# A diffusion step with an S5 scan, a long convolution and a pooling branch: squares summed on TensorE, one normalisation pass over all tokens, filter bias by matmul, and convolution tiles spread evenly beside the scan

## The chip, the cores and the metric

The kernel runs on one core of a Trainium2 chip. The metric is the device time of one execution in microseconds. The kernel before took 1530.49 us, the median of three runs (1528.8 to 1534.48).

## What is computed

One inference step runs 640 tokens (512 latent, 128 context) of width 1024 through two layers. Latents and context have their own conditioning vectors, but share all weights. In outline, for each layer:

```
shift, scale, gate = split(silu(cond) @ w_mod + b_mod)
h = rms_norm(x, norm_g) * (1 + scale) + shift
u_a, g_a, u_b, g_b, u_c, g_c, m = split(h @ w_in)
y_a = glu(gelu(s5_bidirectional(u_a))) * silu(g_a)
y_b = hyena(u_b) * silu(g_b)
y_c = pool(u_c) * silu(g_c)
x = x + gate * ((sigmoid(m_a) * (y_a @ w_br_a) + sigmoid(m_b) * (y_b @ w_br_b)
                 + sigmoid(m_c) * (y_c @ w_br_c)) @ w_out)
```

`hyena` first runs a three-tap convolution over u_b, which gives v, x1 and x2, and then twice z = gate * (long convolution of z with filter h_o, plus z * bias). The filters h_o come from a small MLP over positions, `sin` twice, times a decaying window. `s5_bidirectional` is a complex diagonal recurrence in both directions with 32 groups of 16 channels and 64 states. A final RMS norm ends the step.

## The kernel before

All of it is in fp32 precision: matmuls with the weights W = wh + wl and the data h = hhi + hlo are made of three products in a rounded fp32 form (lines 261 to 263). `split()` makes such a pair: ScalarE rounds (line 238) and VectorE subtracts (line 239). `linear()` streams a weight tile of 128 output channels from memory over SP's DMA queue in two pieces of 256 KB (`wr`), splits each piece, and multiplies with both halves of 320 tokens.

The program is one Python order of calls, from which a scheduler of the framework makes one in-order queue for each engine; it may pull independent instructions of later calls ahead. The stages are:

- **Prologue.** `run()` loads the S5 parameters, runs the filter MLP, computes the S5 discretisation on VectorE (`s5_disc`), squares x0 (`square()`: ScalarE squares a tile, VectorE adds it to an accumulator, line 589), loads the filter's matrices, and makes the modulation in four chunks (`mod_chunk` and `mod_turn`, order 2, 3, 0, 1: chunks 2 and 3 are the scale, 0 and 1 the shift, each for four of the eight channel tiles). A chunk reads 2 MB of w_mod through four buffers `wm` of 512 KB, so four buffers are one chunk. `rinv()` sums the accumulators on TensorE with a column of ones (`ssq`, line 599), takes 1/sqrt by Newton steps on tiny 64x10 tiles, and spreads the result over partitions with a diagonal tile `rdg` and a matmul `rbc`. `make_h()` then makes h: `ht` = x * scale * rr (line 661), `hhi` on ScalarE (line 664), `hlo` on VectorE (line 665); channel tiles 3 and 6 begin on GpSimd (line 656). The half of 320 tokens that holds the boundary of latents and context is done in pieces of 192 and 128. Four calls of `filter()` make the spectra of the long convolution's filters: a matmul over the MLP's output (`fw`, `fwp`), the window (lines 520, 521), the bias added to one row of `hx` and one of `hq` (lines 522, 523), a fold (lines 555 to 559), and matmuls with DFT matrices (`fps`) whose results go to memory (`hd`).
- **Scan stage**, in `layer()`. `u_a` computes the scan's input. Then for each of 8 blocks, `s5_gen` makes matrices: GpSimd and VectorE build `i0`, `i1`, `ow` (lines 873 to 875), TensorE makes `khp` (line 904), ScalarE and VectorE move it to `kh` (lines 906, 907), which goes to memory as `kd` and comes back in a shifted layout as `mt` (line 914). `s5_run` runs the recurrence (`z`, `kk`, `w` on VectorE) and multiplies with `mt` and `ow` into `yp` (lines 974, 976). After each block 3 or 2 tiles of a list `beside` are taken: twelve `conv_u` (TensorE's projection, a copy to `raw`, two VectorE passes of 642 columns, lines 1003 and 1005), four `gate_b` (a gate tile, then two multiplies on GpSimd, line 1034) and four `ahead` (gates put aside in memory). So convolutions fill blocks 0 to 4 (3, 2, 3, 2, 2 of them), and blocks 5 to 7 have none.
- The GLU, four Hyena long convolutions with the pooling branch, the merge of the branches (`merge`, `merge2`), and the output projection.
- **Layer boundary.** Beside the output projection of layer 0 the filters of layer 1 are made; then `rinv` with its Newton steps on GpSimd, `make_h` in two halves, the last two filters, and the `u_a` of layer 1. `s5_vals` clears the tiles `bp` and `bf` (lines 832 and 835) on VectorE.

Of the kernel before, what the change touches and what calls it, by code (L numbers as in the profile page):

```python
# [51 lines left out]
C_ID, C_ONE, C_MT, C_CM, C_DM, C_SEL, C_POSR, C_POSC, C_EL, C_ER, C_PI2, C_EPS, C_MAG, C_N = range(14)  # L52


def _cst_layout():
    sizes = [P, P, NA + NBW, CZ, H, 2, 4 * 8, 4 * 64, 15, 11, 1, 1, 1]
# [166 lines left out]
class Body:  # L223
# [264 lines left out]
    def filter(self, l, o, hf, F, buf=None):  # L488
# [121 lines left out]
    def rinv(self, halves, e, tag="b", root=False):  # L610
# [34 lines left out]
    def make_h(self, l, X, half, rr):  # L645
        nc = self.nc
        sm, sg = self.smod[l]
        t0 = half * HT
        for kk in range(KD):
            t = self.N.tile([P, HT], F32, tag="ht", name="ht", bufs=2)  # L650
            for s, e, _, ci in self.segs(half):
                b = sm[:, kk, ci:ci + 1]
                hi = self.hhi[:, kk, t0 + s:t0 + e]
                lo = self.hlo[:, kk, t0 + s:t0 + e]
                if kk in (3, 6):
                    nc.gpsimd.tensor_tensor(out=t[:, s:e], in0=X[:, kk, t0 + s:t0 + e], in1=rr[:, s:e], op=ALU.mult)
                    nc.scalar.activation(t[:, s:e], t[:, s:e], AF.Identity, scale=sg[:, kk, ci:ci + 1], bias=b)
                    nc.scalar.copy(hi, t[:, s:e])
                    nc.vector.tensor_tensor(out=lo, in0=t[:, s:e], in1=hi.bitcast(F32), op=ALU.subtract)  # L659
# [848 lines left out]
```

## Time and profile before

| | us |
|---|---|
| median of three runs | 1530.49 |
| lowest, highest | 1528.8, 1534.48 |
| the profiled execution | 1534.17 |
| its span in the profile | 1532.4 |
| TensorE busy | 1435.3 (94%) |
| VectorE busy | 1125.5 (73%) |
| ScalarE busy | 672.0 (44%) |
| GpSimd busy | 524.9 (34%) |

The profiled execution is 3.7 us above the median of the runs. Engines are called PE (TensorE), DVE (VectorE), ACT (ScalarE), POOL (GpSimd) and SP (SyncE, which issues the DMAs) in the rows. TensorE's busy share is 94% over the whole, but busy time counts a matmul at half clock as well as one at full clock, and it is not spread evenly: the first 100 us, the two scan stages (about 120 to 340 and 875 to 1090 us) and the layer boundary (800 to 870 us) hold most of what is not busy or runs at a lower granted clock.

### The profile page before, as it was taken

Reading aid. Unit: us, or ns where it says so; the run is one execution under the profiler, and the core shown is the slowest. Engines: PE = TensorE matmul, PEld = TensorE weight load, DVE = VectorE, ACT = ScalarE, POOL = GpSimd, SP = SyncE. Lnnn points to the kernel's source line nnn. Section 1 sums busy time; section 2 is a strip of 40 time slices with the busy share of each in tenths; the row PEclk is TensorE's granted clock in tenths of the full one; section 3 lists DMA queues with packets and bytes.
Section 4 is the critical chain, followed back from the end, with each engine's and each line's share of the span. In section 5 each row is a group of like instructions: output and inputs, shape, how many; then the busy total and the mean of one; then the engine's idle time right before and its main releaser. Section 6 shows DMA issues by size and latency. Waiting matters only on the chain.

```text
span 1532.4 us, 28365 instructions
## 1 busy us (share of the span) xinstructions
PE 1435.3 (94%) x10812; PEld 1372.2 (90%) x10812; DVE 1125.5 (73%) x1951; ACT 672.0 (44%) x1454; POOL 524.9 (34%) x473
## 2 busy tenths in 40 slices
PE   3998899999999999999998897989999999999997
PEld 1688888999999998999997787989999999999996
DVE  8996998854777795555678879896557778866665
ACT  3574545434333342344345644544443334344443
POOL 0033433500343334553323733443003444166401
PEclk9899999999999999999998899999999999999998
DMA  9535122244322246444752342223622223322154
GB/s 313 188 112 132 57 72 70 71 146 123 99 71 77 76 134 234 157 151 139 230 159 81 110 113 68 71 71 94 172 89 81 83 70 106 115 83 83 35 178 153
DMA packets 120464, 178.74 MB, mean 117 GB/s; under 512 B 33944, under 2 KB 58152, under 8 KB 119817
## 3 DMA queue, kind: packets, MB, share of 16 engines
q1 hardware_dynamic: 115737, 170.58, 36.5%
q0 software_dynamic: 1152, 5.77, 1.1%
q8 instruction: 85, 1.39, 0.4%
q10 hardware_dynamic: 3440, 0.59, 0.2%
q14 instruction: 50, 0.41, 0.1%
HBM read 152.71 MB, written 24.18 MB: 115 GB/s over the span
## 4 chain that ended last, share of the span: by engine, by line
PE 68%; DVE 15%; DMA 6%; issue 5%; ACT 3%; SPq 2%; POOL 1%; POOLq 0%; ACTq 0%; DVEq 0%
PE mm L261 15%; PE mm L263 15%; PE mm L262 15%; PE mm L333 3%; PE mm L335 3%; PE mm L334 3%; DVE wl L239 2%; PE inva L1145 1%; SPq L914 1%; DVE i L874 1%; PE invb L1145 1%; PE yp L976 1%; PE modp L404 1%; DVE vx L1003 1%; DVE hlo L665 1%
## 5 line engine op out<-in xcount | busy, mean ns | idle before, releaser
L261 PE MATMUL mm<-hhi,wh 128*128 128x320 f32 x1408 | 446.1, 318 | 15.3 <-ACT raw L996 9.0
L263 PE MATMUL mm<-hhi,wl 128*128 128x320 f32 x1408 | 440.4, 314 | 8.5 <-DVE wl L239 6.3
L262 PE MATMUL mm<-hlo,wh 128*128 128x320 f32 x1408 | 442.4, 314 | 0.5 <-DVE hlo L659 0.4
L239 DVE TENSOR_TENSOR wl<-wr,wh 128x512 fp32r<-128x512 f32 x316 | 265.9, 843 | 114.4 <-ACT wh L238 111.5
L238 ACT CAST wh<-wr 128x512 fp32r<-128x512 f32 x316 | 195.5, 619 | 269.1 <-PE mm L262 188.9
L261 PEld LDWEIGHTS mm<-hhi,wh 128*128 128x128 f32 x1408 | 269.9, 192 | 20.8 <-ACT raw L996 10.0
L263 PEld LDWEIGHTS mm<-hhi,wl 128*128 128x128 f32 x1408 | 269.5, 192 | 9.5 <-DVE wl L239 6.8
L262 PEld LDWEIGHTS mm<-hlo,wh 128*128 128x128 f32 x1408 | 270.1, 192 | 1.7 <-DVE hlo L659 1.2
L262 PE MATMUL mm<-mlo,wh 128*128 128x320 f32 x256 | 79.6, 312 | 0.5 <-DVE mlo L242 0.4
L261 PE MATMUL mm<-mhi,wh 128*128 128x320 f32 x256 | 79.1, 312 | 0.5 <-ACT wh L238 0.4
L263 PE MATMUL mm<-mhi,wl 128*128 128x320 f32 x256 | 78.8, 309 | 0.4 <-DVE wl L239 0.4
L873 POOL TENSOR_TENSOR ow<-cw,po 128x512 f32<-128x512 f32 x32 | 41.9, 1328 | 96.6 <-PE yp L976 96.5
L875 POOL TENSOR_TENSOR i<-i,i 128x1024 f32<-128x1024 f32 x16 | 40.5, 2529 | 100.6 <-DVE i L873 71.8
L1244 DVE SCALAR_TENSOR_TENSOR mth<-mth,mm 128x320 f32<-128x320 f32 x64 | 31.1, 486 | 52.5 <-PE mm L263 52.5
L1246 POOL TENSOR_TENSOR macc<-macc,mth 128x320 f32<-128x320 f32 x32 | 35.0, 1099 | 86.4 <-DVE mth L1244 86.4
L239 DVE TENSOR_TENSOR wl<-ws,wh 128x512 fp32r<-128x512 f32 x48 | 42.7, 889 | 29.7 <-ACT wh L238 28.6
L333 PE MATMUL mm<-hhi,wh 128*128 128x320 f32 x192 | 59.9, 312 | 0.0
L335 PE MATMUL mm<-hhi,wl 128*128 128x320 f32 x192 | 59.4, 309 | 0.0
L334 PE MATMUL mm<-hlo,wh 128*128 128x320 f32 x192 | 59.4, 309 | 0.0
L238 ACT CAST wh<-ws 128x512 fp32r<-128x512 f32 x48 | 29.8, 621 | 60.2 <-PE mm L334 32.3
L1052 POOL TENSOR_TENSOR ps<-pu 128x663 f32<-128x663 f32 x8 | 12.3, 1540 | 120.4 <-ACT pu L1045 120.4
L1246 POOL TENSOR_TENSOR acc<-acc,mth 128x320 f32<-128x320 f32 x32 | 37.7, 1179 | 44.4 <-DVE mth L1244 44.3
(421 smaller groups left out, 3809.9 us busy)
## 6 DMA issues: line engine op xcount, KB each, us to landing
wr<-w_in SPq DMA_DIRECT2D x224, 256.0 KB, 2.6
wm<-w_mod SPq DMA_DIRECT2D x48, 512.0 KB, 5.4
wr<-w_out SPq DMA_DIRECT2D x48, 256.0 KB, 3.0
hd<-hs SPq DMA_DIRECT2D x32, 256.0 KB, 2.3
hsr<-hd SPq DMA_DIRECT2D x32, 256.0 KB, 2.6
mt<-kd SPq DMA_DIRECT2D x128, 32.0 KB, 1.8
wr<-w_br_a SPq DMA_DIRECT2D x16, 256.0 KB, 2.6
wr<-w_br_b SPq DMA_DIRECT2D x16, 256.0 KB, 2.7
```

Of the source, the lines that this page charges most:

```text
L238: nc.scalar.copy(hi, src)
L239: nc.vector.tensor_tensor(out=lo, in0=src, in1=hi.bitcast(F32), op=ALU.subtract)
L261: nc.tensor.matmul(ps[i], wh[:, ks], at(hi, k, sl), start=(k == 0), stop=False)
L262: nc.tensor.matmul(ps[i], wh[:, ks], at(lo, k, sl), start=False, stop=False)
L263: nc.tensor.matmul(ps[i], wl[:, ks], at(hi, k, sl), start=False, stop=(k == kt - 1))
L333: nc.tensor.matmul(out, wh[:, ks], xh, start=(k == 0), stop=False)
L334: nc.tensor.matmul(out, wh[:, ks], xl, start=False, stop=False)
L335: nc.tensor.matmul(out, wl[:, ks], xh, start=False, stop=(k == 3))
L873: eng.tensor_tensor(out=out[:, r], in0=hb(r), in1=pb(0), op=ALU.mult)
L875: e.tensor_tensor(out=out, in0=out, in1=tmp, op=ALU.add)
L1244: v.scalar_tensor_tensor(out=o[:, sl], in0=th[:, sl], scalar=1.0, in1=ps, op0=ALU.add, op1=ALU.mult)
L1246: nc.gpsimd.tensor_tensor(out=acc[:, sl], in0=acc[:, sl], in1=th[:, sl], op=ALU.add)
```

## The change

1. `square_pe()` replaces `square()` in the prologue: ScalarE squares each tile and TensorE sums it straight away into one PSUM tile `ssq` (80 matmuls with one column); the twelve VectorE additions are gone. `rinv` is called before the modulation chunks.
2. `make_h` takes a list of token pieces. In layer 0 it is called once, for 512 latents and 128 context tokens; in layer 1 the halves stay (320, and 192 with 128). `rr` is one tile of 640 columns in both.
3. In `filter()` the bias of the two rows is added by a matmul of one contraction row into the PSUM tiles `fw` and `fwp`, before the window; the constant holds 1/1.05, the inverse of the window at those rows.
4. In layer 1 the Newton steps of `rinv` are on VectorE instead of GpSimd. `rdg` uses the buffers of `sq`.
5. The memsets of `bp` and `bf` are on GpSimd.
6. The list `beside` is rearranged: three convolution tiles alternate with two light tiles (a gate or a tile put aside), tiles 8 to 11 first. Each block still takes 3 or 2; every even block then has two convolutions and one light tile, every odd block one and one.

```
+    def square_pe(self, X, kk, half, ps):
+        nh = HT // 64
+        sq = self.N.tile([P, HT], F32, tag="sq", name="sq", bufs=2)
+        nc.scalar.activation(sq, X[:, kk, half * HT:half * HT + HT], AF.Square)
+        for j in range(nh):
+            c = half * nh + j
+            nc.tensor.matmul(ps[:, c:c + 1], sq[:, j * 64:j * 64 + 64], self.k(C_ONE)[:, 0:1],
+                             start=(half == 0 and kk == 0 and j == 0),
+                             stop=(half == 1 and kk == KD - 1 and j == nh - 1))
...
     filter():
-                                 stop=(i == len(ws) - 1))
+                                 stop=(i == len(ws) - 1 and t not in (2, 4)))
+            if t in (2, 4):
+                r = slice(0, 1) if t == 2 else slice(64, 65)
+                nc.tensor.matmul(fp if t == 4 else fw[:, t], self.k(C_BR)[r], br[r], start=False, stop=True)
...
-        v.tensor_tensor(out=hx[0:1, 2], in0=hx[0:1, 2], in1=br[0:1], op=ALU.add)
-        v.tensor_tensor(out=hq[64:65], in0=hq[64:65], in1=br[64:65], op=ALU.add)
...
     make_h():
-    def make_h(self, l, X, half, rr):
+    def make_h(self, l, X, segs, rr):
-            for s, e, _, ci in self.segs(half):
+            for s, e, ci in segs:
...
     s5_vals():
-            v.memset(t, 0.0)
+            nc.gpsimd.memset(t, 0.0)
...
     run(), prologue:
+                    ssq = self.PS.tile([P, 512], F32, tag="mm", name="ssq", bufs=3)[0:64, 0:2 * (HT // 64)]
-                        self.square(X, kk, 0)
+                        self.square_pe(X, kk, 0, ssq)
-                        self.square(X, kk, 1)
+                        self.square_pe(X, kk, 1, ssq)
                     self.filter_load(0, F, wins, fr, fh)
+                    rr = self.rinv((0, 1), nc.vector, "mm", ps=ssq)
                     self.mod_turn(0, 2, self.mod_chunk(0, 2, M, "mm"), "mm")
                     self.mod_turn(0, 3, self.mod_chunk(0, 3, M, "mm"), "mm")
                     self.s5_disc2(Q, SP, *dd)
                     self.mod_turn(0, 0, self.mod_chunk(0, 0, M, "mm"), "mm")
-                    rr = [r for r, _ in self.rinv((0, 1), nc.vector, "mm")]
                     self.mod_turn(0, 1, self.mod_chunk(0, 1, M, "mm"), "mm")
-                for half in range(2):
-                    self.make_h(0, X, half, rr[half])
+                self.make_h(0, X, ((0, LS, 0), (LS, T, 1)), rr)
...
     run(), layer boundary:
-                            rr = [r for r, _ in self.rinv((0, 1), nc.gpsimd, "mm")]
-                            for half in range(2):
-                                self.make_h(l + 1, X, half, rr[half])
+                            rr = self.rinv((0, 1), nc.vector, "mm")
+                            self.make_h(l + 1, X, ((0, HT, 0),), rr)
+                            self.make_h(l + 1, X, ((HT, LS, 0), (LS, T, 1)), rr[:, HT:])
...
     layer():
-            beside = [lambda i=i: self.conv_u(l, i, vx[i // 4][:, i % 4, :], SP) for i in range(12)]
-            beside += [lambda i=i: self.gate_b(l, i, S, vx[2]) for i in range(4)]
-            beside += [lambda i=i: self.ahead(l, 40 + i, AF.Tanh, 0.5, SP) for i in range(4)]
+            heavy = [lambda i=i: self.conv_u(l, i, vx[i // 4][:, i % 4, :], SP) for i in (*range(8, 12), *range(8))]
+            gates = [lambda i=i: self.gate_b(l, i, S, vx[2]) for i in range(4)]
+            ahead = [lambda i=i: self.ahead(l, 40 + i, AF.Tanh, 0.5, SP) for i in range(4)]
+            light = ahead[:2] + gates + ahead[2:]
+            beside = []
+            for i in range(4):
+                h, g = heavy[3 * i:3 * i + 3], light[2 * i:2 * i + 2]
+                beside += [h[0], g[0], h[1], h[2], g[1]]
```

The change moves instructions in the queues that the scheduler makes. In the following rows, lines of the changed kernel from about 640 on are 16 higher.

**SP's queue in the prologue.** `wm` are the pieces of w_mod, `hd` the filters' results on their way to memory, `wr` weights of the first projection. Before:

```order
L252 DMA wr<-w_in 128x512 x3
L401 DMA wm<-w_mod 128x1024 x4
L252 DMA wr<-w_in 128x512 x2
L401 DMA wm<-w_mod 128x1024 x2
L252 DMA wr<-w_in 128x512
L401 DMA wm<-w_mod 128x1024 x2
L496 DMA br<-hyb 1x256 x2
L401 DMA wm<-w_mod 128x1024 x4
L544 DMA hd_66<-hs 128x512 x4
```

With the change:

```order
L547 DMA hd_66<-hs 128x512 x3
L498 DMA br<-hyb 1x256 x2
L547 DMA hd_66<-hs 128x512
L403 DMA wm<-w_mod 128x1024 x4
L547 DMA hd_66<-hs 128x512
L403 DMA wm<-w_mod 128x1024 x2
L547 DMA hd_66<-hs 128x512
L403 DMA wm<-w_mod 128x1024 x2
L547 DMA hd_66<-hs 128x512 x2
L403 DMA wm<-w_mod 128x1024 x3
L547 DMA hd_66<-hs 128x512
L403 DMA wm<-w_mod 128x1024
```

All of w_mod was asked for ahead of the filters' results; now the last three chunks stand among the results of filters 0 and 1. On PE, likewise, the first chunk's matmuls stand behind `rbc` instead of ahead of the filters.

**VectorE's queue in the scan of layer 0, up to block 2's `kh`.** Before:

```order
L873 TENSOR_TENSOR i_2321<-bb,pi 128x512 x2
L1003 SCALAR_TENSOR_TENSOR vx_1052<-raw,par_143,vx_1052 128x642
L981 SCALAR_TENSOR_TENSOR gu<-gu,yp 128x324
L1005 SCALAR_TENSOR_TENSOR vx_1052<-raw,par_143,vx_1052 128x642
L874 TENSOR_TENSOR i_2604<-bb,pi 128x512 x2
L983 SCALAR_TENSOR_TENSOR gy<-gu,yp 128x324
L989 MEMSET raw 128x1
L907 SCALAR_TENSOR_TENSOR kh<-cst,par_143,khp 128x16
```

With the change:

```order
L889 TENSOR_TENSOR i_2307<-bb,pi 128x512 x2
L997 SCALAR_TENSOR_TENSOR gu<-gu,yp 128x324
L923 SCALAR_TENSOR_TENSOR kh<-cst,par_143,khp 128x16
L999 SCALAR_TENSOR_TENSOR gy<-gu,yp 128x324
L969 TENSOR_TENSOR z<-pz,tt 128x656
L970 TENSOR_TENSOR t_2058<-pz,tt 128x656
L890 TENSOR_TENSOR i_2585<-bb,pi 128x512 x2
```

A convolution's two passes (lines 1003 and 1005) and the pair `i1` stood between `i0` and `kh`; they are not there now, and `i1` comes behind the scan's `z`.

**VectorE's queue at the layer boundary, up to the first `ht`.** `fb`, `hx`, `hc` and `hq` are parts of two filters. Before:

```order
L239 TENSOR_TENSOR flp<-hq,fhp 128x256
L239 TENSOR_TENSOR flo<-hc,fhi 128x512
L522 TENSOR_TENSOR fb<-fb,br 1x256
L557 SCALAR_TENSOR_TENSOR fb<-fb 128x256
L632 TENSOR_TENSOR rdg<-cst,ry 64x320 x2
L559 SCALAR_TENSOR_TENSOR hc<-hx,hc 128x512
L239 TENSOR_TENSOR flo<-hc,fhi 128x512
L556 SCALAR_TENSOR_TENSOR fb<-fb 128x256
L558 SCALAR_TENSOR_TENSOR fb<-fb 128x512
L559 SCALAR_TENSOR_TENSOR fb<-fb 128x512
L239 TENSOR_TENSOR flo<-hc,fhi 128x512
L661 SCALAR_TENSOR_TENSOR ht<-X,sg_6689,rr 128x320 x2
```

With the change:

```order
L561 SCALAR_TENSOR_TENSOR fb<-fb 128x512
L620 TENSOR_TENSOR rt<-rt,rx 64x10
L241 TENSOR_TENSOR flo<-hc,fhi 128x512
L562 SCALAR_TENSOR_TENSOR fb<-fb 128x512
L621 TENSOR_SCALAR rt<-rt 64x10
L526 TENSOR_TENSOR hq<-fwp,wins 128x256
L241 TENSOR_TENSOR flo<-fb,fhi 128x512
L622 TENSOR_TENSOR ry<-ry,rt 64x10
L241 TENSOR_TENSOR flp<-hq,fhp 128x256
L648 TENSOR_TENSOR rdg<-cst,ry 64x320 x2
L241 TENSOR_TENSOR flo<-fb,fhi 128x512 x2
L678 SCALAR_TENSOR_TENSOR ht<-X,sg_6690,rr 128x320 x2
```

The Newton steps (`rt`, `ry`) are now in VectorE's queue, one by one between the filters' folds, and `rdg` stands behind these folds instead of in the midst of them.

## Rows read from the trace of the kernel before

**Rows 1.** Engines' busy time in five stretches; then PE's granted clock, DMA share, GB/s.
```profile
0.00:45.00 45.00, 18.27 (x64) 7.55 (x65) 38.50 (x144) 15.82 (x33) 1.47 (x6) 0.92 0.96 322
120.00:200.00 80.00, 69.79 (x662) 67.25 (x661) 66.51 (x94) 38.18 (x98) 29.97 (x17) 0.98 0.35 92
200.00:280.00 80.00, 75.58 (x695) 73.58 (x693) 70.87 (x99) 42.16 (x106) 33.59 (x20) 0.94 0.26 74
280.00:360.00 80.00, 77.73 (x665) 76.49 (x664) 50.52 (x67) 33.66 (x77) 15.43 (x15) 0.98 0.45 129
860.00:940.00 80.00, 66.57 (x622) 63.96 (x623) 70.69 (x89) 42.60 (x111) 39.60 (x23) 0.94 0.31 84
```

The five busy times of a row are PE, PE's weight loads, DVE, ACT and POOL, each with its count of instructions.

**Rows 2.** Timeline of DVE in the prologue: start, duration (us), instruction, [idle before <-releaser].
```profile
8.46 0.20 DVE L707 TENSOR_SCALAR ex<-sp 128x64 f32<-128x64 f32 x1 [5.30 <-DMA sp<-s5p]
...
68.34 0.89 DVE L632 TENSOR_TENSOR rdg<-cst,ry 64x320 f32<-64x320 f32 x2
...
79.41 1.00 DVE L661 SCALAR_TENSOR_TENSOR ht<-X,sg,rr 128x320 f32<-128x320 f32 x2
...
85.83 0.68 DVE L661 SCALAR_TENSOR_TENSOR ht<-X,sg,rr 128x192 f32<-128x192 f32 x2
...
107.14 0.28 DVE L659 TENSOR_TENSOR hlo<-ht,hhi 128x128 fp32r<-128x128 f32 x1
```

**Rows 3.** Groups of DVE, 0 to 110 us: count | busy us, mean ns | idle before.
```profile
L589 DVE TENSOR_TENSOR acc<-acc,sq 128x320 f32<-128x320 f32 x12 | 5.8, 483 | 0.0
...
L558 DVE SCALAR_TENSOR_TENSOR hc<-hx,hc 128x512 f32<-128x512 f32 x4 | 2.8, 688 | 0.0
...
L523 DVE TENSOR_TENSOR hq<-hq,br 1x256 f32<-1x256 f32 x4 | 1.7, 417 | 0.1
...
L522 DVE TENSOR_TENSOR hx<-hx,br 1x256 f32<-1x256 f32 x4 | 1.6, 408 | 0.0
```

**Rows 4.** The DMAs of `wm`, 0 to 110 us: SP's own wait before issuing, and landing.
```profile
DMA wm<-w_mod: 14.4, 7
...
DMA to landing us min/median/max: 4.1/4.7/5.4
```

**Rows 5.** PE's waits, 130 to 350 us: total us, times, longest.
```profile
PE yp L974 <- DMA mt<-kd: 8.0, 4, 3.6
PE mm L261 <- ACT raw L996: 5.1, 2, 3.1
```

**Rows 6.** PE's waits, 875 to 1090 us.
```profile
PE yp L974 <- DMA mt<-kd: 11.5, 5, 3.7
PE mm L261 <- ACT raw L996: 3.9, 2, 2.6
```

**Rows 7.** Timeline of PE in the scan of layer 0, two waits.
```profile
198.52 0.41 PE L261 MATMUL mm<-hhi,wh 128*128 128x320 f32 x1 [3.06 <-ACT raw L996]
...
258.21 0.69 PE L974 MATMUL yp<-ug,mt 128*128 128x81 f32 x2 [3.63 <-DMA mt<-kd]
```

**Rows 8.** Timeline of DVE ahead of the `kh` of block 2, layer 0.
```profile
185.96 2.76 DVE L1003 SCALAR_TENSOR_TENSOR vx<-raw,par,vx 128x642 f32<-128x642 f32 x1 [0.46 <-ACT vx L1001]
...
190.24 4.37 DVE L874 TENSOR_TENSOR i<-bb,pi 128x512 f32<-128x512 f32 x2
...
194.94 0.22 DVE L907 SCALAR_TENSOR_TENSOR kh<-cst,par,khp 128x16 f32<-128x16 f32 x1
194.96 0.06 DVE L989 MEMSET raw<- 128x1 f32 x1
```

**Rows 9.** Groups of POOL, 130 to 350 us: the gates' multiplies.
```profile
L1034 POOL TENSOR_TENSOR vx<-vx,sgb 128x512 f32<-128x512 f32 (+1 forms) x8 | 9.8, 1247 | 10.8 <-ACT sgb L1026 10.8
```

**Rows 10.** Timelines of POOL and DVE at the layer boundary.
```profile
809.23 0.20 POOL L626 TENSOR_SCALAR ry<-rx 64x10 int32<-64x10 int32 x1 [12.51 <-ACT rx L625]
...
817.30 0.88 DVE L632 TENSOR_TENSOR rdg<-cst,ry 64x320 f32<-64x320 f32 x2
...
844.62 0.48 DVE L832 MEMSET bp<- 128x512 f32 x1
```

More of the change, by code (lines that the diff above doesn't have):

```diff
@@ L50 @@
 GELU_C = math.sqrt(2.0 / math.pi)
[L52 removed]
+C_ID, C_ONE, C_MT, C_CM, C_DM, C_SEL, C_POSR, C_POSC, C_EL, C_ER, C_PI2, C_EPS, C_MAG, C_BR, C_N = range(15)
 def _cst_layout():
[L56 removed]
+    sizes = [P, P, NA + NBW, CZ, H, 2, 4 * 8, 4 * 64, 15, 11, 1, 1, 1, P]
     offs = np.concatenate([[0], np.cumsum(sizes)])
@@ L116, in constants @@
     cst[:, CO[C_MAG]] = MAGIC
+    for r in (0, 64):
+        cst[r, CO[C_BR] + r] = 1.0 / (1.0 + f32(0.05))
     fmax = 15
@@ L629, in rinv @@
         prs = []
+        rt = None if root else self.N.tile([P, HT * len(halves)], F32, tag="rr", name="rr", bufs=1)
         for i in range(len(halves)):
-            dg = self.N.tile([P, nh, 64], F32, tag="ht", name="rdg", bufs=2)[0:64]
+            dg = self.N.tile([P, nh, 64], F32, tag="sq", name="rdg", bufs=2)[0:64]
             nc.vector.tensor_tensor(out=dg, in0=self.ident[0:64, 0:64].unsqueeze(1).to_broadcast([64, nh, 64]),
@@ L652, in make_h @@
                 b = sm[:, kk, ci:ci + 1]
-                hi = self.hhi[:, kk, t0 + s:t0 + e]
-                lo = self.hlo[:, kk, t0 + s:t0 + e]
+                hi = self.hhi[:, kk, s:e]
+                lo = self.hlo[:, kk, s:e]
+                tv, rv = t[:, s - base:e - base], rr[:, s - base:e - base]
                 if kk in (3, 6):
[L656 to L659, printed above, removed]
+                    nc.gpsimd.tensor_tensor(out=tv, in0=X[:, kk, s:e], in1=rv, op=ALU.mult)
+                    nc.scalar.activation(tv, tv, AF.Identity, scale=sg[:, kk, ci:ci + 1], bias=b)
+                    nc.scalar.copy(hi, tv)
+                    nc.vector.tensor_tensor(out=lo, in0=tv, in1=hi.bitcast(F32), op=ALU.subtract)
@@ L660, in make_h @@
                     continue
-                nc.vector.scalar_tensor_tensor(out=t[:, s:e], in0=X[:, kk, t0 + s:t0 + e],
-                                               scalar=sg[:, kk, ci:ci + 1], in1=rr[:, s:e], op0=ALU.mult,
-                                               op1=ALU.mult)
-                nc.scalar.activation(hi, t[:, s:e], AF.Identity, bias=b)
-                nc.vector.scalar_tensor_tensor(out=lo, in0=t[:, s:e], scalar=b,
-                                               in1=hi.bitcast(F32), op0=ALU.add, op1=ALU.subtract)
+                nc.vector.scalar_tensor_tensor(out=tv, in0=X[:, kk, s:e], scalar=sg[:, kk, ci:ci + 1], in1=rv,
+                                               op0=ALU.mult, op1=ALU.mult)
@@ L668, in u_a @@
+                nc.scalar.activation(hi, tv, AF.Identity, bias=b)
+                nc.vector.scalar_tensor_tensor(out=lo, in0=tv, scalar=b, in1=hi.bitcast(F32),
+                                               op0=ALU.add, op1=ALU.subtract)
     def u_a(self, l, S, uas):
```

16 lines of the change are left out of this document (9 added, 7 removed).

## The prediction

> **What bounds the kernel now.** I read the busy time by stretches first. TensorE is near its limit over most of the span, so an edit on another engine pays only where TensorE waits or runs at a lower granted clock. Two kinds of place are left. In the first 45 us TensorE is busy for 18.27 us and VectorE for 38.50 [rows 1]; VectorE's timeline shows that it waits for the S5 parameters until 8.46 us [rows 2], and from there it is packed. The prologue is VectorE's: `rdg` at 68.34, then `ht` and `hlo` mixed with the filters, the last `hlo` at 107.14, and behind it the u_a that the scan needs. In the scan stages TensorE and VectorE are close to each other: 69.79 and 66.51 of 80 us, then 75.58 and 70.87; in layer 1, 66.57 and 70.69; only where the convolutions have run out does VectorE fall to 50.52 [rows 1]. TensorE's waits there have two names, `mt` from memory and `raw` on ScalarE: 8.0 + 5.1 = 13.1 us in layer 0 [rows 5], 11.5 + 3.9 = 15.4 us in layer 1 [rows 6].
>
> VectorE's queue is behind both. Ahead of block 2's `kh` stand a convolution pass of 2.76 us from 185.96 and an `i1` pair of 4.37 us, and the tiny `kh` of 0.22 us comes at 194.94 [rows 8]. From it the path leads through two trips to memory to `mt`. The clearing of `raw` stands right behind `kh`, at 194.96, and TensorE then waits 3.06 us for that `raw` at 198.52; two blocks later it waits 3.63 us for `mt` [rows 7].
>
> **The change, part by part, against the profiled 1534.2 us** (3.7 above the median).
>
> *Prologue.* Neighbours on VectorE overlap by about 0.08 us: two 320-wide `ht` take 1.00 where one 192 and one 128 take 0.68 [rows 2], so I take off 0.08 from each mean. Twelve additions go: 12 x (0.483 - 0.08) = 4.8 us. Eight bias rows go: 8 x (0.41 - 0.08) = 2.7 us [rows 3]. `make_h` had three pieces, 0.50 + 0.68 = 1.18 us; it now has 512 at 0.688 [rows 3] and 128 at 0.28 [rows 2], about 0.96 with their overlap counted in full. There are 14 such chains on VectorE (six `ht`, eight `hlo`): 14 x 0.22 = 3.1 us. Together 10.6 us of a queue that has no holes. What was hidden there stays hidden: the memsets lie in the 5.30 us wait for the parameters [rows 2], and the forty more one-column matmuls and eight bias matmuls lie on TensorE, which idles more than half of the opening.
>
> The step is not free. w_mod's last three chunks, 6 MB, can now be asked for only when the first chunk's matmuls have freed the buffers, which stand behind `rbc`. `rdg` moves up by the additions and by the filter work it no longer waits for, about 10 us, to some 58. If the chunks stream at the opening's 322 GB/s [rows 1], 6.3 MB take 19.5 us, and the last shift is there near 79. If each chunk goes as two pairs of 5.4 us, the slowest landing [rows 4], it is 3 x 10.8 = 32 us, near 91. Some 7 us of VectorE's work remain behind the last shift (four `ht` and `hlo` chains with their 0.96 us each, plus a split), so the last `hlo` comes at 97 by VectorE's own work (107.1 - 10.6), and at 98 by the late shift. I take 9 us gained, with 3 to 12 as bounds.
>
> *Scan, each layer.* Convolutions per block go from 3, 2, 3, 2, 2, 0, 0, 0 to 2, 1, 2, 1, 2, 1, 2, 1. VectorE's total is the same, but its queue ahead of `kh` is shorter where it was long. In block 2 the order shows one convolution's two passes and the `i1` pair behind `kh`; by the rows they were most of the 9 us between 185.96 and 194.94 [rows 8]. The two waits of [rows 7], 6.7 us, belong to blocks 2 and 4 and should go; of the other 6.4 us, that of block 5, whose queue is shorter too, should go and those of block 1, whose queue is as long as before, stay. I count 9 of the 13.1. Blocks 5 to 7 get a pass or two ahead of their `kh`, and I give back 3. PEclk was 0.98, 0.94 and 0.98 in the three stretches: 80 x (0.02 + 0.06 + 0.02) = 8 us of clock at most; its lower stretches lie beside waits, and I count 2. Layer 0 gains 9 - 3 + 2 = 8. Layer 1 has 15.4 us of waits of the same names and 80 x 0.06 = 4.8 us of clock in its first stretch; I take 8 again. Bounds for each: nothing gained, or all waits and half of the clock, 13.1 + 4 = 17.
>
> The gates come earlier in the list (blocks 2 to 5). Their eight multiplies on GpSimd are 9.8 us [rows 9], now beside the fuller half of VectorE's scan. In row 8 the same kind of `i1` takes 4.37 us for two instructions where GpSimd works beside it; a 512-wide pass elsewhere takes 0.688 [rows 3]. So VectorE loses time to GpSimd in this kernel. The Trainium skill (SBUF — State Buffer, "SBUF: two separate sides") says that a VectorE instruction with two SBUF inputs and a GpSimd instruction that reads SBUF exclude one another for a whole instruction. The trace agrees: 4.37 against 1.4 us. By that rule the gates could cost VectorE up to their 9.8 us in the blocks where its queue decides; that is the rival of the other sign below.
>
> *Layer boundary.* Newton on GpSimd starts at 809.23 and `rdg` follows at 817.30 [rows 10], 8 us for thirteen tiny steps and a fold. On VectorE a step is short, but the steps are spread between the folds of two filters and `rdg` stands behind them all: it comes 2 to 4 us later than now, while the work that followed it is done by then. Four bias rows, 4 x 0.33 = 1.3 us, and the 1.5 us of memsets from 844.62 leave VectorE. I take 2 us gained, bounds 5 lost and 5 gained.
>
> Sum: -9 - 8 - 8 - 2 = -27, so 1507 against 1534.2; moved by 3.7 to the median, **1504 us**.
>
> **The rivals.**
> *The waits move, they don't go.* From `kh` to `mt` is memory, and with a convolution in every block each `kh` has something ahead of it. For: blocks 1 and 5 waited with short queues. Against: in blocks 6 and 7 of before, with none ahead, TensorE didn't wait. Then only 9 + 2 are left: 1530.5 - 11 = 1519.
> *The modulation is late.* The three chunks take 32 us or more beside 256 KB results that SP sends in between, in order; SP waited 14.4 us for `wm` buffers even before [rows 4]. With the last shift at 100, the prologue gains nothing; the scans and boundary give 18: 1512. With both, 1528: the change then does nothing.
> *Slower, by GpSimd.* If the gates' multiplies block VectorE in blocks 2 to 5, and the convolutions in 5 to 7 make those blocks wait too, then six of eight blocks each lose a wait of 3.6 us, the longest that there was [rows 5]: 21.6 against 13.1 now, 8.5 lost in each layer, plus 2 of clock in each. That is 21 lost, 11 gained: 1540. It decides where `kh` is over some 7 us behind the end of `khp` in most blocks.
> *More than forecast.* All waits and half of the clock go in both layers: 9 + 17 + 17 + 2 = 45: 1486.
>
> **How the numbers follow.** A measurement can tell about 0.5%, 7.7 us, from no change. Forecast, 1493 to 1513: 0.52. Waits move, 1514 to 1523: 0.20. Modulation late, to 1512 or, with the other, to 1528: 0.12. Slower: 0.07. More: 0.09. The range reaches from 1490 to 1525 and leaves out half of the better case, the slower one and the worst of the mixed one. Faster by over 0.5% is below 1522.8: the forecast, the better case, most of the second (0.15) and half of the third (0.06), together 0.82. Within 0.5% is the rest of these two, 0.11. Slower: 0.07.
>
> **What the profile of the changed kernel would show.** Prologue: no additions at line 589's place, `rdg` before 60 us, the last `hlo` at 96 to 99; if TensorE waits for `wm` over 5 us behind `rbc`, the second rival is at work. Scan: TensorE's waits on `mt` and `raw` at 4 to 7 us a layer, PEclk 0.97 or more in the second stretch, `kh` of blocks 2 and 4 within 4 us of `khp`, that of 5 to 7 no later than 5. Boundary: `rdg` about 2 us later after `rx`, but `hlo` finished 1 to 3 us sooner. The forecast is wrong if the waits of the scan hold their 13 and 15 us, or if the prologue's end stays at 107.

## The result

The changed kernel is slower, by about 0.6%: 1540.2 us, the median of seven runs (1537.55 to 1546.45), against 1530.86 us for the kernel before beside it (seven runs). The ratio is 1.0062 with an interval of 1.0036 to 1.0087. I had forecast 1504 us and 1490 to 1525.

The profiled execution took 1540.2 us with a span of 1538.4, 6.0 us more than the span before. This is where the same event of the program stands in the two timelines (microseconds, from the first row of the named instruction):

```
                                          before    after   later by
rdg, layer 0                               68.34    56.52    -11.8
last smod (modulation), layer 0            77.87    99.83    +22.0
last hlo, layer 0                         107.14   114.89     +7.8
first pz of the scan, layer 0             144.99   153.41     +8.4
first plp (pooling), behind that scan     399.96   403.76     +3.8
rx, layer boundary                        808.87   814.29     +5.4
rdg, layer boundary                       817.30   829.00    +11.7
first khp of the scan, layer 1            883.38   893.44    +10.1
first plp behind that scan               1149.26  1154.25     +5.0
last matmul rbc                          1524.11  1529.96     +5.9
```

The prologue lost 8 us where I expected 9 gained. The stretch from the first pooling matmul to the scan of layer 1, with the boundary in it, lost 6 (3.8 us late become 10.1), where I expected 2 gained. The scans took up part of it: behind the first, 8.4 us late have become 3.8, behind the second, 10.1 have become 5.0.

**The prologue after.** VectorE's timeline: start, duration, instruction, idle before. These rows answer to [rows 2].

```profile
56.52 0.88 DVE L648 TENSOR_TENSOR rdg<-cst,ry 64x320 f32<-64x320 f32 x2
...
69.23 0.17 DVE L420 TENSOR_TENSOR smod<-modt,par 128x8 f32<-128x8 f32 x1 [1.19 <-PE modt L417]
...
79.74 0.17 DVE L420 TENSOR_TENSOR smod<-modt,par 128x8 f32<-128x8 f32 x1 [0.34 <-PE modt L417]
...
90.52 0.17 DVE L420 TENSOR_TENSOR smod<-modt,par 128x8 f32<-128x8 f32 x1 [0.51 <-PE modt L417]
...
99.83 0.16 DVE L420 TENSOR_TENSOR smod<-modt,par 128x8 f32<-128x8 f32 x1
...
114.89 0.28 DVE L676 TENSOR_TENSOR hlo<-ht,hhi 128x128 fp32r<-128x128 f32 x1
```

`rdg` comes at 56.5, as the additions' removal promised. Then everything waits for the modulation, one chunk every 9 to 11 us. SP's timeline shows why: the pieces of w_mod's last three chunks are asked for in groups of four to one between 63 and 86 us, as matmuls of the chunk before have freed their buffers and as the filters' results in the same queue let them pass. The first four groups:

```profile
63.21 1.77 SPq L403 DMA_DIRECT2D wm<-w_mod  x4
...
70.22 1.98 SPq L403 DMA_DIRECT2D wm<-w_mod  x2
...
74.23 1.98 SPq L403 DMA_DIRECT2D wm<-w_mod  x2
...
80.72 3.06 SPq L403 DMA_DIRECT2D wm<-w_mod  x3
```

TensorE did not idle in this time, which I had thought it would. Two stretches of the changed kernel, columns as in [rows 1]:

```profile
0.00:45.00 45.00, 30.27 (x184) 24.26 (x185) 36.08 (x136) 17.82 (x37) 2.96 (x10) 1.00 0.80 256
...
200.00:280.00 80.00, 75.42 (x720) 73.23 (x719) 69.15 (x93) 40.85 (x106) 43.43 (x27) 1.00 0.25 74
```

In the first 45 us TensorE was busy for 18.27 us [rows 1] and is now for 30.27. The chain of waits from 55 us on (start, duration, what) names TensorE's `fw`, `modp` and `modt`, with the new bias matmuls of line 517 among them; among its longest pieces none is VectorE's until 101.75. Four of them:

```profile
64.04 1.49 PE fw L513 x6
65.53 0.62 PE fw L517 x2
...
68.41 0.79 PE modt L417 x8
69.19 0.98 PE modp L406 x4
```

**The scans after.** TensorE's waits in 130 to 350 us, which answer to [rows 5]:

```profile
PE yp L990 <- DMA mt<-kd: 6.1, 3, 2.9
PE yp L992 <- DVE w L984: 3.5, 4, 1.6
PE mm L263 <- ACT raw L1012: 2.5, 3, 1.2
PE yp L990 <- issue: 2.4, 1, 2.4
```

and in 885 to 1100 us, which answer to [rows 6]:

```profile
PE yp L990 <- DMA mt<-kd: 4.2, 2, 2.7
PE mm L263 <- ACT raw L1012: 3.5, 3, 1.7
PE yp L992 <- DVE w L984: 2.8, 2, 1.6
PE yp L990 <- issue: 1.5, 2, 1.3
```

`mt` and `raw` fell from 13.1 to 8.6 us and from 15.4 to 7.7. New names stand beside them: `yp` waits for VectorE's `w`, 3.5 and 2.8 us (0.2 and 0.5 before), and 2.4 and 1.5 us more for which the profile names no releaser.

Behind the fall is `kh`, as predicted. In block 2 it comes 3.3 us behind the start of `khp` (from TensorE's and VectorE's timelines):

```profile
193.83 0.97 PE L920 MATMUL khp<-ow,bp 128*32 128x112 f32 x32
197.12 0.22 DVE L923 SCALAR_TENSOR_TENSOR kh<-cst,par,khp 128x16 f32<-128x16 f32 x1
```

Before, it was 10.4 us (184.55 to the 194.94 of [rows 8]). In block 4 it is 3.2 us (248.52 to 251.74) instead of 8.1 (242.78 to 250.91).

A table from one execution each is good to some 3 us: the changed kernel and that of experiment 3 are the same up to the boundary, and the last `yp` of their first scans stands at 343.7 and 346.5.

### The profile page after: what moved, and what is told of

Read it like the earlier page. It is cut to its first block, busy times and chain, and to the rows that moved or that the text cites. A ratio compares the mean times of both kernels' runs of the same rounds, so it can differ in the third digit from the quotient of the medians.

```text
span 1538.4 us, 28629 instructions
## 1 busy us (share of the span) xinstructions
PE 1464.7 (95%) x10964; PEld 1390.9 (90%) x10964; DVE 1101.2 (72%) x1914; ACT 671.3 (44%) x1444; POOL 522.9 (34%) x466
## 3 DMA queue, kind: packets, MB, share of 16 engines
q1 hardware_dynamic: 115737, 170.64, 36.2%
## 4 chain that ended last, share of the span: by engine, by line
PE 69%; DVE 14%; DMA 6%; issue 5%; ACT 3%; POOL 2%; SPq 1%; POOLq 0%; DVEq 0%; ACTq 0%
PE mm L265 14%; PE mm L263 14%; PE mm L264 14%; PE mm L335 3%; PE mm L337 3%; PE mm L336 3%; DVE wl L241 2%; PE modp L406 2%; PE inva L1161 1%; PE invb L1161 1%; PE fw L513 1%; PE yp L992 1%; DVE i L890 1%; DVE kk L978 1%; DVE kk L977 1%
## 5 line engine op out<-in xcount | busy, mean ns | idle before, releaser
L265 PEld LDWEIGHTS mm<-hhi,wl 128*128 128x128 f32 x1408 | 269.0, 191 | 11.9 <-DVE wl L241 10.1
L889 POOL TENSOR_TENSOR ow<-cw,po 128x512 f32<-128x512 f32 x32 | 38.6, 1223 | 102.8 <-PE yp L992 102.7
L891 POOL TENSOR_TENSOR i<-i,i 128x1024 f32<-128x1024 f32 x16 | 44.1, 2758 | 71.3 <-DVE i L889 67.8
```

Source lines behind the costliest of these rows:

```text
L265: nc.tensor.matmul(ps[i], wl[:, ks], at(hi, k, sl), start=False, stop=(k == kt - 1))
L889: eng.tensor_tensor(out=out[:, r], in0=hb(r), in1=pb(0), op=ALU.mult)
L891: e.tensor_tensor(out=out, in0=out, in1=tmp, op=ALU.add)
```

## Experiments

Each was timed in five rounds beside the kernel before (medians between 1529.89 and 1531.73 us in the four batches).

**1. rinv back behind the third chunk, in the changed kernel.** `e1` moves one line:

```
-                    rr = self.rinv((0, 1), nc.vector, "mm", ps=ssq)
                     self.mod_turn(0, 2, self.mod_chunk(0, 2, M, "mm"), "mm")
...
                     self.mod_turn(0, 0, self.mod_chunk(0, 0, M, "mm"), "mm")
+                    rr = self.rinv((0, 1), nc.vector, "mm", ps=ssq)
```

> The changed kernel with one line moved: rinv of layer 0 back behind the third modulation chunk. Theory A (rinv's place keeps the chunks' matmuls, and with them w_mod's buffers, behind rbc, so the last shift comes at 99.8 us instead of 77.9): the last smod comes before 85 us, the last hlo at 96 to 103 instead of 114.9, and the time falls by 10 to 18 us, to 1522 to 1530. Rival (the modulation is late only because TensorE and ScalarE are slowed by the filters themselves): the last hlo stays over 110 and the time falls by less than 4 us.

Measured: 1547.84 us, 1.0115 (1.0091 to 1.014), so 8 us slower still than the changed kernel. The modulation did as expected (last `smod` at 83.8) and the last `hlo` came at 104.5, just above the range; the time did not follow. The order had changed too: the first `khp` now stood behind some 265 projection matmuls instead of 192, and came at 157.5 us (138.1 in the changed kernel, 126.6 before). So the last `hlo` alone is not what the scan's start hangs on. Theory A and its rival both miss; TensorE's own work had to be looked at.

**2. Bias on VectorE, in the changed kernel.**

```
-            if t in (2, 4):
-                r = slice(0, 1) if t == 2 else slice(64, 65)
-                nc.tensor.matmul(fp if t == 4 else fw[:, t], self.k(C_BR)[r], br[r], start=False, stop=True)
...
+        v.tensor_tensor(out=hx[0:1, 2], in0=hx[0:1, 2], in1=br[0:1], op=ALU.add)
+        v.tensor_tensor(out=hq[64:65], in0=hq[64:65], in1=br[64:65], op=ALU.add)
```

> The changed kernel with the filter bias added on VectorE again. Theory A (a bias row by matmul costs TensorE 0.75 us, twice in a filter, and TensorE is the bound beside layer 0's output projection and at the boundary): fw to the next tile takes 1.2 us again instead of 2.7, and four filters of layer 1 give back 4 to 6 us: 1534 to 1536; the prologue moves by less than 2. Rival (VectorE is the bound at the boundary, as I predicted, and the four rows of 0.34 us are worth more there): no gain, or up to 3 us slower.

Measured: 1535.6 us, 1.0037 (1.0026 to 1.0049), 4.6 less than the changed kernel; the two intervals overlap, so the size is uncertain. It is what theory A gives, but its "the prologue moves by less than 2" misses: the last `hlo` of layer 0 came at 108.65 instead of 114.89, so layer 0's filters had their part in it (6 and 12 tell how much the bias costs in either layer, in the kernel before).

**3. Newton on GpSimd, in the changed kernel.**

```
-                            rr = self.rinv((0, 1), nc.vector, "mm")
+                            rr = self.rinv((0, 1), nc.gpsimd, "mm")
```

> The changed kernel with layer 1's Newton steps on GpSimd again. Theory A (on VectorE the thirteen steps stand between the folds of two filters, so rdg comes 14.7 us after rx, on GpSimd 8.4): rdg 8 to 10 us after rx, the boundary 3 to 6 us shorter: 1534 to 1537. Rival (rdg is early, but ht waits for the folds in VectorE's queue all the same): the last hlo and the time move by less than 2 us.

Measured: 1538.94 us, 1.0054 (1.0039 to 1.0069). `rdg` came 8.7 us after `rx` (817.22, 825.89) instead of 14.7, and the last `hlo` 36.2 us after it instead of 40.2: the boundary is shorter as theory A says. The time is above its range, though: the medians differ by 1.3 us only, and the two intervals overlap, so what is left of the 4 us at the end isn't told apart from nothing.

**4. The old list beside the scan, in the changed kernel.**

```
-            heavy = [lambda i=i: self.conv_u(...) for i in (*range(8, 12), *range(8))]
...
+            beside = [lambda i=i: self.conv_u(l, i, vx[i // 4][:, i % 4, :], SP) for i in range(12)]
+            beside += [lambda i=i: self.gate_b(l, i, S, vx[2]) for i in range(4)]
+            beside += [lambda i=i: self.ahead(l, 40 + i, AF.Tanh, 0.5, SP) for i in range(4)]
```

> The changed kernel with the old list beside the scan (twelve convolutions, then gates, then tiles put aside). Theory A (the new list gives back 7.7 us in layer 0 and 5.1 in layer 1 between the first khp and the stage behind the scan): TensorE's waits for mt and raw go up to 12 to 16 us a layer, and the time rises by 9 to 14 us: 1549 to 1554. Rival (the scans took up the late start because the first blocks have slack, whatever the list): the time moves by less than 4 us.

Measured: 1543.59 us, 1.0088 (1.0074 to 1.0102), 3.4 above the changed kernel. The waits for `mt` and `raw` did come back as theory A says, to 13.7 and 14.6 us, but the time lies with the rival (and the interval overlaps the changed kernel's). So the length of these two waits is not their price, and part of what the scans take up in the table above is the slack of a scan that starts late.

**5. The new list alone, in the kernel before.**

```
-            beside = [lambda i=i: self.conv_u(l, i, vx[i // 4][:, i % 4, :], SP) for i in range(12)]
...
+            beside = []
+            for i in range(4):
+                h, g = heavy[3 * i:3 * i + 3], light[2 * i:2 * i + 2]
+                beside += [h[0], g[0], h[1], h[2], g[1]]
```

> The kernel before with the new list beside the scan and nothing else. Theory A (the list is worth what the changed kernel's scans took up, 7.7 + 5.1 us): 1516 to 1521, the waits for mt and raw of TensorE 4 to 8 us a layer. Rival (putting the old list into the changed kernel cost 3.4 us only, so that is what the list is worth; the rest of the 12.8 us was slack behind a late start): 1525 to 1529.

Measured: 1522.97 us, 0.9953 (0.9936 to 0.9969): 7.0 us faster. This part does what it was made for, at half of the 16 us that I gave it. In its profile the scan of layer 0 is 4.5 us ahead of before at the stage behind it, and the end 7.25. TensorE's waits for `mt` and `raw` are 4.8 us in layer 0 and 7.3 in layer 1 (13.1 and 15.4 before), while those for `w` have grown to 4.4 and 4.3: half of what goes comes back under another name.

**6. The bias by matmul alone.** The kernel before with the new matmuls in `filter()`, and rr as one tile (7).

```
+                nc.tensor.matmul(fp if t == 4 else fw[:, t], self.k(C_BR)[r], br[r], start=False, stop=True)
...
-        v.tensor_tensor(out=hx[0:1, 2], in0=hx[0:1, 2], in1=br[0:1], op=ALU.add)
-        v.tensor_tensor(out=hq[64:65], in0=hq[64:65], in1=br[64:65], op=ALU.add)
```

> The kernel before with the filter bias by matmul (and rr as one tile), everything else as before. Theory A (sixteen such matmul pairs put about 0.6 us each, 9.7 us, on TensorE, which is bound by its work nearly everywhere; VectorE's 5.3 us are saved where they count less): 4 to 8 us slower, 1534 to 1538. Rival (the cost shows only with the other parts): within 2 us of before.

Measured: 1545.72 us, 1.0099 (1.0078 to 1.012), 15.7 us slower: twice the most that theory A gave, and the rival is out. It is the dearest part. Its prologue (VectorE's and TensorE's timelines) against [rows 2]:

```profile
78.27 0.88 DVE L648 TENSOR_TENSOR rdg<-cst,ry 64x320 f32<-64x320 f32 x2
```

```profile
74.73 1.22 PE L517 MATMUL fw<-br,cst 1*128 1x256 f32 x2
75.87 1.22 PE L513 MATMUL fw<-w,fh 64*128 64x256 f32 x2
```

A bias matmul of one contraction row takes as long as one of 64 rows beside it: 1.22 us here. VectorE waited 9.0 us for `fhi` and 6.5 us for `fw` and `fwp` between 36 and 92 us. TensorE's granted clock was 0.58 in 45 to 60 us and 0.65 in 60 to 75, where the kernel with rr as one tile (7) has 0.89 and 0.77:

```profile
60.00:75.00 15.00, 15.00 (x93) 12.41 (x93) 7.10 (x24) 4.48 (x9) 0.00 (x0) 0.65 0.37 139
```

The last `hlo` came at 120.05. The chain of waits from 36 to 125 us is led by TensorE's `fw` and `modp` (13.8 and 12.9%), where before it is led by VectorE's `hlo` (9.7%): in this kernel TensorE bounds the prologue. How much of the 15.7 us is the added matmuls themselves, and how much the lower clock, no run separates.

**7. rr as one tile, alone.**

```
+        rt = None if root else self.N.tile([P, HT * len(halves)], F32, tag="rr", name="rr", bufs=1)
-            dg = self.N.tile([P, nh, 64], F32, tag="ht", name="rdg", bufs=2)[0:64]
+            dg = self.N.tile([P, nh, 64], F32, tag="sq", name="rdg", bufs=2)[0:64]
```

> The kernel before with only rr as one 640-wide tile and rdg in sq's buffers; the same work on every engine. It changes the scheduler's order at a few places (the first khp comes 17 projection matmuls later). Theory A (order changes that move no work between engines are worth under 3 us): within 3 us of before. Rival (the order of the first block's khp decides, as the first experiment suggests, where it was 74 matmuls late): 4 us slower or more.

Measured: 1528.21 us, 0.9987 (0.9974 to 1.0001), as theory A says. A baseline for experiments 6, 8, 9, 11 and 12, whose edits build on it. This change of order costs and gains next to nothing in time. It does move VectorE's end of the prologue: with the same 24 `hlo` steps, the last one starts at 100.0 us (the second of this row of its timeline) instead of 107.14 [rows 2].

```profile
99.66 0.68 DVE L680 SCALAR_TENSOR_TENSOR hlo<-ht,smod,hhi 128x192 fp32r<-128x192 f32 x2
```

Yet its first `yp` came at 149.3 us (147.1 before). So 7 us less at the end of VectorE's queue were worth next to nothing here. Its profile also shows how far order and chance move one stage: with the old list, 249.9 us lie between the first `pz` and the first `plp` of layer 0, as many as in experiment 5 with the new one (255.0 before).

**8. rinv early alone.** The kernel before with squares still on VectorE, rr as one tile, and

```
+                    rr = self.rinv((0, 1), nc.vector, "mm")
                     self.mod_turn(0, 2, self.mod_chunk(0, 2, M, "mm"), "mm")
...
                     self.mod_turn(0, 0, self.mod_chunk(0, 0, M, "mm"), "mm")
-                    rr = self.rinv((0, 1), nc.vector, "mm")
```

> The kernel before with rinv of layer 0 called ahead of the modulation chunks, squares still added on VectorE. Theory A (rinv's place pushes the chunks behind rbc, each chunk then takes some 10 us in a row of buffer, landing, matmul and shift): last smod near 100 us, last hlo 112 to 118 instead of 107.1, the time 5 to 10 us more. Rival (it is the squares on TensorE that make the modulation late): the last smod before 85 us and the time within 3 us of before.

Measured: 1544.41 us, 1.0091 (1.0071 to 1.0111), 14.4 us slower. VectorE's timeline has the four late `smod` of the changed kernel again (73.09, 80.47 and these two), with no square on TensorE:

```profile
92.41 0.17 DVE L420 TENSOR_TENSOR smod<-modt,par 128x8 f32<-128x8 f32 x1
...
101.76 0.17 DVE L420 TENSOR_TENSOR smod<-modt,par 128x8 f32<-128x8 f32 x1 [3.16 <-PE modt L417]
```

The late modulation of theory A is shown, and costs more than it said: the last `hlo` came at 122.9, beyond its 112 to 118, and the time is over its 10 us. Part of it may be TensorE's speed: its filter matmuls took nearly twice as long until 60 us (last section). How much that adds, no run separates.

**9. The squares alone.** The kernel before with rinv in its old place, rr as one tile, and for each half

```
-                        self.square(X, kk, 0)
+                        self.square_pe(X, kk, 0, ssq)
```

> The kernel before with the squares of layer 0 summed by TensorE, rinv in its old place (and rr as one tile), all else as before. Theory A (eighty one-column matmuls between 16 and 37 us run TensorE at its lower speed, and it stays there to about 50 us, so that the filters' and the chunks' matmuls take twice as long; TensorE becomes the bound of that stretch): a filter matmul of 256 columns starts 0.21 us behind the one before until 50 us or later, the twelve additions are won back on VectorE and lost again; the time within 4 us of the kernel with rr as one tile (1528), to either side. Rival (the lower speed is hidden, VectorE bounds the prologue): last hlo 4 to 5 us earlier, the time 1523 to 1525.

Measured: 1537.15 us, 1.0038 (1.0022 to 1.0055), 5.4 us above the kernel before in its batch and, by the two ratios, 8 above experiment 7. Twelve additions fewer on VectorE, and slower: the last `hlo` at 108.0, 8 us later than in experiment 7. It is theory A's side (the filter matmuls start 0.21 us apart until 66 us), but its "within 4 us" is too little.

**10. The squares, make_h in one pass, the memsets and the list.** The changed kernel with the edits of 1, 2 and 3 together:

```
+                    rr = self.rinv((0, 1), nc.vector, "mm", ps=ssq)
...
+        v.tensor_tensor(out=hx[0:1, 2], in0=hx[0:1, 2], in1=br[0:1], op=ALU.add)
...
+                            rr = self.rinv((0, 1), nc.gpsimd, "mm")
```

> The changed kernel with three parts undone at once: rinv back behind the third chunk, bias on VectorE, Newton on GpSimd. What is left are the squares on TensorE, make_h in one pass, the memsets and the new list. Theory A (of the losses the bias and rinv's place are the large ones, some 13 us each in the prologue, overlapping): the prologue ends no later than before, the scans give their 7 us: 1517 to 1524. Rival (the squares on TensorE cost as much as they did with the bias, where rinv's old place alone made it 8 us slower): 1530 to 1540.

Measured: 1529.59 us, 0.9982 (0.9966 to 0.9999). Between the two: theory A is over 5 us too low, the rival just missed. It differs from experiment 1 by the bias and Newton, and is 18 us faster. It differs from experiment 11, timed beside it, by the squares and `make_h` in one pass, and is 3.5 us slower. VectorE's timeline has the last `hlo` near where I had predicted it, at 97:

```profile
58.33 0.89 DVE L647 TENSOR_TENSOR rdg<-cst,ry 64x320 f32<-64x320 f32 x2
...
96.22 1.01 DVE L680 SCALAR_TENSOR_TENSOR hlo<-ht,smod,hhi 128x512 fp32r<-128x512 f32 x2
```

Even so the first `yp` of the scan came at 160.6 us (147.1 before). So an early end of VectorE's queue is worth nothing by itself, as in 7. A reading that fits: TensorE had been doing projections of channel tiles that were ready, and has them, and the squares' matmuls, to do all the same (the first `khp` stands behind some 265 projection matmuls here, 192 before).

**11. List, memsets and rr's tile.** Nothing that adds work to TensorE: experiment 7 with the list of 5 and

```
-            v.memset(t, 0.0)
+            nc.gpsimd.memset(t, 0.0)
```

> The kernel before with the new list beside the scan, the memsets on GpSimd and rr as one tile: nothing that adds work to TensorE and no change of order in the prologue. Theory A (gains of separate places add up: 7.0 for the list, 1.8 for the tile and up to 1.5 for the memsets at the boundary): 1519 to 1522, faster than both kernels. Rival (the gain of rr's tile was in the scan's order, which the new list changes anyway): 1522 to 1525.

Measured: 1526.06 us, 0.9962 (0.9943 to 0.9981). Faster than both kernels, but theory A misses, and it is no better than the list alone (0.9953): the small gains do not add up. Against experiment 7 (0.9987) the list and the memsets together are worth some 4 us.

**12. The bias by matmul in layer 1 only.** Experiment 6 with

```
...
-            if t in (2, 4):
+            if l and t in (2, 4):
...
+        if l == 0:
+            v.tensor_tensor(out=hx[0:1, 2], in0=hx[0:1, 2], in1=br[0:1], op=ALU.add)
+            v.tensor_tensor(out=hq[64:65], in0=hq[64:65], in1=br[64:65], op=ALU.add)
```

> The kernel before (with rr as one tile) with the filter bias by matmul in layer 1 only; layer 0's filters add it on VectorE. Theory A (in the run with the bias by matmul in both layers, some 13 of the 15.7 us arose in the prologue, where TensorE ran at its lower speed from 64 to 83 us, and the four filters of layer 1 cost 2 to 5): 1530 to 1533, that is 2 to 5 us over the kernel with rr as one tile. Rival (the matmuls cost in proportion to their number, half in each layer): 1535 to 1538.

Measured: 1533.12 us, 1.0017 (1.0006 to 1.0029), some 5 over experiment 7, the upper end of theory A. Experiment 6 stands some 17 over experiment 7, so layer 0's four filters cost about 12 us and layer 1's about 5.

## Why the prediction was wrong

**The first step that failed** is a clause: "the forty more one-column matmuls and eight bias matmuls lie on TensorE, which idles more than half of the opening." I had priced what left VectorE, row by row, and what came to TensorE at nothing, by a busy share of the first 45 us. The count was off too: the changed kernel has 80 one-column matmuls where the kernel before has 20, sixty more (each stands in the profile as two records, 160 and 40). At the end of that stretch and behind it TensorE is part of the chain (`fw`, `fps`, `modp`, `modt`), and VectorE waits for it. TensorE's groups of the changed kernel in 0 to 120 us show the size of what came:

```profile
L602 PE MATMUL ssq<-cst,sq 128*64 128x1 f32 x160 | 17.7, 246 | 4.4 <-ACT sq L599 4.4
...
L517 PE MATMUL fw<-br,cst 1*128 1x256 f32 x8 | 3.8, 567 | 0.0
L517 PE MATMUL fwp<-br,cst 1*128 1x256 f32 x8 | 3.3, 497 | 0.0
```

17.7 us of squares (before, `rsum` had some 3 us) and 7.1 us of bias, in a stretch that I had called VectorE's. Alone, the squares cost 5 to 8 us (experiment 9; 3.5 with `make_h` in one pass, 10 beside 11) and the bias of layer 0 some 12 (6, 12). Layer 1's bias I had not priced at all on TensorE, only four of the eight rows that VectorE loses, 1.3 us. Two of its four filters lie beside the output projection, where TensorE has no hole, the other two behind `rx`. The timeline beside the projection:

```profile
774.85 0.28 PE L513 MATMUL fw<-w3l,fs 128*128 128x256 f32 x1
775.06 0.69 PE L517 MATMUL fw<-br,cst 1*128 1x256 f32 x2
775.68 0.39 PE L513 MATMUL fw<-w3h,fs 128*128 128x256 f32 x1
...
776.35 0.69 PE L517 MATMUL fwp<-br,cst 1*128 1x256 f32 x2
776.97 0.41 PE L263 MATMUL mm<-mhi,wh 128*128 128x320 f32 x1
```

From the first `fw` matmul to the next projection matmul it is now 2.7 us (774.25 to 776.97); before it was 1.2 (770.46 to 771.65). Four such filters are 6 us of TensorE, against 8 x 0.33 us taken from VectorE; 5 us were measured (12).

**The second** is the modulation. The rival was named, its mechanism is the one that the profile and experiment 8 show, and its condition, the last shift at 100, is what came (99.83); I gave it 0.12. My own step had the last shift near 79 or near 91, because I had counted w_mod's transfers. The chunks also stand in TensorE's queue between the filters, and in SP's between the results, and each waits for the chunk before: 9 to 11 us each. Its price I put at the prologue's 9 us gained becoming nothing; alone it cost 14.4 us.

**The delays do not add up.** Bias alone costs 15.7 us, rinv early alone 14.4, the squares alone 5 to 8, and in the changed kernel the whole is 9.3 slower with the list's 7 gained. Undoing one of them there gives back 4.6 us (2) or makes it worse (1); undoing both, with Newton, 10.6 (10). So in part they lie over one another; which covers which is not settled.

**The boundary** lost 6 us where I said 2 gained. `rdg` came 14.7 us behind `rx`, for 8.4 before; I had written 2 to 4 us later, it was 6. By experiment 3 that is 4 us of the boundary's trace, of which the medians show 1.3. The bias of layer 1, 5 us alone, is the larger part by the times. How the two share the 6 us is not settled: from `rx` to the first `khp` the traces show 74.5 us before and 79.2 after, 74.4 without Newton on VectorE (3), 78.1 without the bias (2), but 80.5 with the bias alone in layer 1 (12).

**The scans** were right in mechanism: `kh` moved forward, and the waits for `mt` and `raw` fell. I said 4 to 7 us left a layer; it was 8.6 and 7.7. The size, 8 us a layer, was double or more: 7.0 us for both in the kernel before (experiment 5), some 4 with the memsets on top of 7 (11), 3.4 in the changed kernel (4). I had let "blocks 5 to 7" give back 3 and overlooked `w`, for which `yp` waits 3 us a layer now, and over 4 in experiment 5. That GpSimd's multiplies would decide did not happen: its busy time in 200 to 280 us rose from 33.59 [rows 1] to 43.43 us, and TensorE's waits fell. The Trainium skill (SBUF — State Buffer, "SBUF: two separate sides") says that a VectorE instruction with two SBUF inputs and a GpSimd instruction that reads SBUF exclude one another for a whole instruction. The trace of before agrees: the pair `i0` took 1.29 us at 184.22, with GpSimd idle until 185.65, and the pair `i1` of the same shape 4.37 us beside GpSimd's work [rows 8]. It was not what made the kernel slower: the list that moves the gates is a gain by itself (5). That rival's figure, 1540, is the measured one by chance only.

**VectorE's sum**, 10.6 us less and a last `hlo` at 97, looks right in experiment 10, which has it at 96 to 97. That is luck in part: experiment 7, with none of the additions and bias rows gone, has it at 100, so no more than 3 of the 10 us can be put down to the sum. The 3.1 us of `make_h` in one pass were not tried alone. And what the sum stood for was wrong: the end of VectorE's queue does not set the end of the stage (7, 10).

## What to carry to other kernels

Work that is moved to another engine has to be priced there, in the stretch in which it lands and in the order of that queue, with the same care as what it frees; a busy share over the stretch does not show that the engine is on the chain. Here a one-row matmul took as long as one of 64 rows (1.22 us each in experiment 6), so a bias row is cheap on VectorE (0.33 us) and dear on a bound TensorE (some 0.75 us). Moving a step forward in program order also moves whatever shares its queue or its buffers backward: look first for who waits behind it, here 6 MB of weights through four buffers.

## What was not expected of the hardware

In the changed kernel TensorE ran at the lower of its two levels (1.2 instead of 2.4 GHz) until 53 us, though the granted clock of these stretches reads 1.00. The level is read here from the time that one shape takes. TensorE's timeline and the stretch of 45 to 60 us:

```profile
10.33 2.47 PE L463 MATMUL mlpp<-zt,w 33*128 33x320 f32 x4 [10.33 <-DMA w<-hyw]
...
29.76 3.34 PE L602 MATMUL ssq<-cst,sq 128*64 128x1 f32 x30
...
50.27 0.41 PE L554 MATMUL fps<-fhp,frp 128*128 128x256 f32 x1
50.49 0.41 PE L552 MATMUL fps<-fhp,frp 128*128 128x256 f32 x1
...
56.94 0.28 PE L553 MATMUL fps<-flo,fr 128*128 128x256 f32 x1
57.05 0.28 PE L554 MATMUL fps<-fhi,fr 128*128 128x256 f32 x1
...
60.84 1.34 PE L651 MATMUL rbc<-rdg,cst 64*128 64x320 f32 x4
```

```profile
45.00:60.00 15.00, 15.00 (x60) 10.71 (x59) 13.06 (x33) 8.56 (x20) 0.00 (x0) 1.00 0.25 68
```

Filter matmuls of one shape start 0.21 us apart at 50 us and 0.12 at 57; the records of the squares take 0.11 us each at 30 us. The lower level is where the program starts: four records of 320 columns take 2.47 us at 10 us, in the kernel before too, and 1.34 at 61. What differs is when TensorE leaves it. In the kernel before it had by 31 us, where the eight `modt` took 1.05 us, as they did at 57; with squares between w_mod's first matmuls (experiment 9) they took 1.86 at 37.

The eighty squares are not needed for the late rise. Experiment 8 has only the twenty one-column matmuls of before, ten at 26 us and ten at 42, reads 1.00 as well, and has the long steps until 60 us:

```profile
51.47 0.41 PE L553 MATMUL fps<-fhp,frp 128*128 128x256 f32 x1
51.68 0.41 PE L551 MATMUL fps<-fhp,frp 128*128 128x256 f32 x1
...
60.69 0.28 PE L552 MATMUL fps<-flo,fr 128*128 128x256 f32 x1
60.81 0.28 PE L553 MATMUL fps<-fhi,fr 128*128 128x256 f32 x1
```

They can put it off, though: experiment 9 differs from 7 by them alone and by what the scheduler made of it, and has 0.21 us until 66 where 7 has 0.12 from 51.7 to 55.7. In 8 and in the changed kernel w_mod's first matmuls have moved behind `rbc`; in 9 the squares stand between them. In the kernel before and in 7 they run from 26 us with nothing between them, and the level has risen by 31. No run changed that alone, so what brings the rise is not shown.

The level also fell again in the kernel before. Forty one-column records ran 0.06 us apart at first, and the filter matmuls behind them, which had been 0.12 us apart at 52 us, went to 0.21 until 66 us; there the granted clock shows it:

```profile
58.31 0.74 PE L599 MATMUL ssq<-cst,acc 128*64 128x1 f32 x10
58.91 0.72 PE L599 MATMUL ssq<-cst,sq 128*64 128x1 f32 x10
...
61.89 0.41 PE L549 MATMUL fps<-fhi,fr 128*128 128x256 f32 x1
62.10 0.41 PE L550 MATMUL fps<-flo,fr 128*128 128x256 f32 x1
```

```profile
60.00:75.00 15.00, 15.00 (x89) 11.86 (x89) 12.92 (x35) 6.89 (x15) 0.00 (x0) 0.77 0.14 54
```

So in these traces the durations of one shape tell the level more surely than the granted clock of a stretch. Why the bias alone had TensorE at the lower level from about 46 to 58 and from 64 to 81 us (experiment 6) stays open.
